# RWKV-7 and attention trunk: tiles for the first half's r mixes, the place of two loads, and the order inside a head norm

## The chip, the cores and the metric

One core of a Trainium2 chip runs the whole program. The metric is the device time of one execution in microseconds. The engines have their own instruction queues: PE (TensorE) multiplies matrices, DVE (VectorE), ACT (ScalarE) and POOL (GpSimd) work elementwise, SP (SyncE) issues most of the loads and stores. An engine works through its queue in order, so an instruction that waits holds up all that stand behind it.

## The reference, cut to what matters

Two layers over a sequence of S = 512 rows with D = 1024 features. Layer 0 is an RWKV-7 layer, and it is there that the change lies:

```
h = rms_norm(x)                       # h_prev is h shifted by one row
xr, xw, xk, xv, xa, xg = h + (h_prev - h) * mu[0..5]
r = xr @ w_r;  k = xk @ w_k;  v = xv @ w_v
w = -softplus(-(w0 + tanh(xw @ w1) @ w2)) - 0.5     # w1: 1024 x 64, w2: 64 x 1024
a = sigmoid(a0 + (xa @ a1) @ a2)                     # a1, a2 likewise
g = sigmoid(xg @ g1) @ g2
y = scan over the rows, 16 heads of 64, state 64 x 64 per head
y = head_norm(y) * lnx_w + lnx_b + bonus             # per head of 64: the "head norm"
x = x + (y * g) @ w_o
```

After it come a SwiGLU FFN, one shared K/V projection, a layer of differential attention and a second FFN. The change touches none of these.

## The kernel before, in words

Activations lie feature by feature on the partitions, as 8 tiles (kt = 0 to 7) of 128 features by 512 rows. The 16 heads are 8 pairs, and the layer works in two halves of four pairs: the first half's projections take columns 0 to 511 of a weight, the second half's the rest. A product in full precision is split in three: weight and activation are each cast to a high part (ACT) and a remainder (DVE), and TensorE adds high x high, low x high and high x low (L156 to L158).

The start: four loads of x (two on SP's queue, two on ACT's), squares (L265, L267) and a chain of additions on DVE (L272), a product with ones (L281), an inverse square root, the row factors (L254), and the normed h (L452). Also loaded there are `cst`, `lw` (lnx_w, broadcast over 128 partitions, 0.5 MB; on SP, L461, ahead of the first w_r load; it is read in the head norm, L904) and `sel` (on POOL's queue, L465).

The first stage merges four generators in turn (L480): the norming of h, the w product (into bank `ca`), the a product (into bank `cb`) and the first half of r (`r_half(0)`, which runs proj_p). Each of the last three needs its own mix of each feature tile: ACT scales h (L372), DVE adds the shifted h (L373). For w and a one fp32 product follows (L392, two instructions). For r, ACT casts the mix (L199), DVE makes the remainder (L200) and twelve products follow (L156 to L158, four banks). The weights of r come in four loads through one rotating `wr` buffer (the other two of three hold w1 and a1), with a cast L195 and a remainder L196 each. All mixes of this stage take the tag `xm`, which has two buffers: a mix waits until the mix two before it has been used. Mixes for k take the tag `xk`, which has nine.

The joint: when both products are done, ACT takes tanh of `ca` (L477) and copies both results (L399), DVE makes the remainders (L400), and TensorE multiplies by w2 and a2 (L414, L415), which ACT evicts (L538). Then the first half of k runs as proj_p again, with its own L195, L196, L199, L200.

After that a plan by numbers interleaves pairs, solve and the recurrence with the second halves of r, k and v. The recurrence hands over its output in tiles of 128 rows, four for each half; each of these eight gets a head norm (head_out, L879): mean and variance per head (L884 to L891, with the square on ACT, L888), inverse square root, weight and bonus (L904, L906), and then four turns of 128x128 (L911), each followed by its ACT copy with bias (L912), all in one PSUM bank `cb`. Behind the last of them the tail of the layer begins: DVE multiplies by g (L642), ACT casts (L646), DVE makes a remainder (L648), the weight w_o is cast (L662), and the last projection runs (L156).

A scheduler of the framework places instructions within each engine's queue; buffers and banks decide what waits.

Of the kernel before, what the change touches and what calls it, by code (L numbers as in the profile page):

```python
# [18 lines left out]
P = 128  # L19
D = 1024  # L20
# [22 lines left out]
class Trunk:  # L43
# [394 lines left out]
    def rwkv(self, turn):  # L438
        nc, A = self.nc, self.A
        xT = self.h  # L440
        rstd = self.norm_cols(xT, "pr", True)
        bc = self.rows_bc(rstd, "pr")
        cp = self.cp
        self.omu = cp.tile([P, 6 * KT], F32, name="omu")
        i0 = VI["mu0"] * KT
        nc.vector.tensor_scalar(self.omu, self.par[:, i0:i0 + 6 * KT], -1.0, 1.0, op0=ALU.mult, op1=ALU.add)
        h = xT

        def normed():
            for j in range(KT):  # L450
                v = h[j // 2][:, j % 2, :]
                nc.vector.scalar_tensor_tensor(out=v, in0=v, scalar=self.vec("g_mix0", j), in1=bc, op0=ALU.mult, op1=ALU.mult)  # L452
                yield
        self.h = h
        self.Dc = cp.tile([P, NP, NCH], F32, name="Dc")
        self.bon = cp.tile([P, NT, NP, 2], F32, name="bon")
        self.rkc = cp.tile([P, NP, 2], F32, name="rkc")
        for p in range(NP):
            nc.vector.tensor_scalar(self.rkc[:, p, :], self.cst[:, C_BO:C_BO + 2], self.vec("r_k", p), None, op0=ALU.mult)
        self.lw = cp.tile([P, D], F32, name="lw")  # L460
        nc.sync.dma_start(self.lw, A["lnx_w"].broadcast_to([P, D]))  # L461
        self.v_d = self.dr.tile([2, 2, S, 4, C], F32, name="v_d")
        self.st_d = self.dr.tile([2, NCH, P, 4, 8 * C], F32, name="st_d")
        self.sel = cp.tile([P, NT, P], F32, name="sel")
        nc.gpsimd.dma_start(self.sel, A["sel"])  # L465
        self.R, self.Pt, self.kept = {}, {}, {}
        self.oT = {}

        pwa = []

        def low(i):
            def out(ps):
                pwa or pwa.append(self.T("s", [P, 2, S], F32R))
                if i:
                    return self.halves(pwa[0][:, 1, :], ps)
                t = self.T("pr", [P, S])
                nc.scalar.activation(t, ps, AF.Tanh)  # L477
                self.halves(pwa[0][:, 0, :], t)
            return out
        self.merge(*zip((normed(), self.lora(h, 1, [(A["w1"], 2)], low(0), "ca"), self.lora(h, 4, [(A["a1"], 2)], low(1), "cb"), self.r_half(0)),  # L480
                        self.START))
        sg, aa = self.rates(pwa[0], 0)
        kr, ld, pg, sa, x1 = ([], []), ([], []), [], [(sg, aa)], []
        self.drain(self.k_half(0, kr[0]))

        def rates():
            sa.append(self.rates(pwa[0], 1))
            yield

        def out(w):  # L490
            if w == 0:
                x1.extend(self.load_x())
            yield from self.out_half(w, pg, x1)
        t = self.TIMES
        self.plan(
            [(lambda: self.pairs(0, kr[0], *sa[0], ld[0]), 20, *t["pairs0"]), (lambda: self.solve(0, *ld[0]), 36, *t["solve0"]),
             (lambda: self.rec(0), 24, *t["rec0"])],
            [(lambda: self.r_half(1), 8, *t["r1"]), (lambda: self.k_half(1, kr[1]), 8, *t["k1"]), (rates, 1, t["k1"][1], t["k1"][1]),
             (lambda: self.v_half(0), 8, *t["v0"]), (lambda: self.v_half(1), 8, *t["v1"]), (lambda: self.gate(pg), 8, *t["gate"]),
             (lambda: out(0), 9, *t["out0"])],  # L500
            [(lambda: self.pairs(1, kr[1], *sa[1], ld[1]), 20, *t["pairs1"]), (lambda: self.solve(1, *ld[1]), 36, *t["solve1"]),
             (lambda: self.rec(1), 24, *t["rec1"])])
        turn()
        self.drain(out(1))
        return x1

    def mixes(self, key, m, w):

        kept = self.kept.setdefault(key, {})

        def mix(kt):
            if key == "r":
                return self.mix_tile(self.h, m, kt)
            if w:
                return kept.pop(kt)
            x = kept[kt] = self.mix_tile(self.h, m, kt, "xk")
            return x
        return mix
# [360 lines left out]
    def head_out(self, w, tt, y):  # L879
        nc = self.nc  # L880
        w4 = w * 4
        yf = y.rearrange("p a b c -> p (a b) c")
        mean = self.tiny([P, 8])
        nc.vector.tensor_reduce(out=mean, in_=yf, axis=AX.X, op=ALU.add)  # L884
        nc.vector.tensor_scalar(mean, mean, 1.0 / C, None, op0=ALU.mult)
        self.lo("yf").tensor_tensor(out=yf, in0=yf, in1=mean.unsqueeze(2).to_broadcast([P, 8, C]), op=ALU.subtract)
        sq = self.T("ho", [P, 8, C])
        nc.scalar.activation(sq, yf, AF.Square)  # L888
        var = self.tiny([P, 8])
        nc.vector.tensor_reduce(out=var, in_=sq, axis=AX.X, op=ALU.add)  # L890
        nc.vector.tensor_scalar(var, var, 1.0 / C, 64e-5, op0=ALU.mult, op1=ALU.add)  # L891
        yield
        vt = self.T("ho", [P, 2, 4, C])
        for par in range(2):
            nc.sync.dma_start(vt[:, par], self.v_d[w, par, tt * P:(tt + 1) * P])
        for par in range(2):
            self.lo("vt").tensor_tensor(out=vt[:, par], in0=vt[:, par], in1=self.bon[:, tt, w4:w4 + 4, par:par + 1].to_broadcast([P, 4, C]), op=ALU.mult)
        rs = self.tiny([P, 8])
        self.rsqrt_v(rs, var, "ty")
        nc.vector.tensor_tensor(out=yf, in0=yf, in1=rs.unsqueeze(2).to_broadcast([P, 8, C]), op=ALU.mult)  # L900
        lv = self.lw[:, w * 512:w * 512 + 512].rearrange("p (a b c) -> p b a c", b=2, c=C)
        yo = sq.rearrange("p (a b) c -> p a b c", b=2)
        for par in range(2):
            nc.vector.tensor_tensor(out=y[:, par], in0=y[:, par], in1=lv[:, par], op=ALU.mult)  # L904

            nc.vector.tensor_tensor(out=yo[:, :, par, :], in0=y[:, par], in1=vt[:, par], op=ALU.add)  # L906
        yield
        ps = self.bank("cb")
        for i in range(4):
            p = w4 + i  # L910
            nc.tensor.transpose(ps[:, i * P:(i + 1) * P], yo[:, i].rearrange("p a b -> p (a b)"), self.ident)  # L911
            nc.scalar.activation(self.oT[p // 2][:, p % 2, tt * P:(tt + 1) * P], ps[:, i * P:(i + 1) * P], AF.Identity, bias=self.vec("lnx_b", p))  # L912

    def ffn(self, xT, l, tag, out=None):
# [367 lines left out]
```

## Time and profile before

| what | value |
|---|---|
| runs of the kernel, us | 1516.05, 1524.76, 1524.42 (median 1524.42) |
| profiled execution, us | 1518.63 |
| its span, us | 1516.8 |
| mean granted clock of TensorE | 0.984 |
| PE busy | 1447.9 us, 95% |
| DVE busy | 787.3 us, 52% |
| ACT busy | 529.1 us, 35% |
| POOL busy | 187.3 us, 12% |

The span runs from the first to the last record of the profiled execution. "Idle before" is the time in which the engine stood still ahead of an instruction, and the arrow names what ended it. The granted clock is 1.00 at 2.4 GHz and 0.50 at 1.2 GHz.

### The profile page before, as it was taken

How to read it: one execution, taken by the hardware profiler on the slowest of the kernel's cores; microseconds unless marked ns; L12 is line 12 of the kernel's file. 1: busy time of each engine (PE TensorE's matmuls, PEld its weight loads, DVE VectorE, ACT ScalarE, POOL GpSimd, SP SyncE). 2: the span in 40 equal slices, each digit the busy share in tenths (PEclk: the TensorE clock that was granted, in tenths of full speed). 3: DMA queues.
4: the chain of work that ended last, by engine and by line, in shares of the span. 5: the costliest groups of instructions: out<-in, count | busy, mean ns of one | idle time of the engine just before them, and what ended most of it. 6: DMA issues, size and time to landing. Idle time of an engine off the chain costs nothing.

```text
span 1516.8 us, 23107 instructions
## 1 busy us (share of the span) xinstructions
PE 1447.9 (95%) x9576; PEld 1140.0 (75%) x9576; DVE 787.3 (52%) x1511; ACT 529.1 (35%) x926; POOL 187.3 (12%) x156
## 2 busy tenths in 40 slices
PE   3899999999997999999999989999999999999998
PEld 2465555767685788888888879988778888888887
DVE  6735549677666644433323276666665444443222
ACT  4652341213423433222222153556654323232111
POOL 0002313100000111111100023111001111111000
PEclk9989999999998999999999999999999999999999
DMA  5112423776321322222222222111112232322231
GB/s 159 57 69 93 165 105 107 281 241 207 133 89 42 116 96 85 98 97 97 96 93 96 95 92 84 59 68 43 42 43 97 96 99 92 102 91 100 98 122 64
DMA packets 59162, 155.82 MB, mean 103 GB/s; under 512 B 12848, under 2 KB 19248, under 8 KB 57008
## 3 DMA queue, kind: packets, MB, share of 16 engines
q1 hardware_dynamic: 57856, 152.76, 29.3%
q8 instruction: 75, 1.23, 0.3%
q10 hardware_dynamic: 1120, 1.32, 0.3%
q14 instruction: 31, 0.25, 0.1%
q0 software_dynamic: 80, 0.26, 0.0%
HBM read 133.34 MB, written 20.97 MB: 102 GB/s over the span
## 4 chain that ended last, share of the span: by engine, by line
PE 83%; DVE 9%; ACT 3%; POOL 2%; issue 1%; DMA 1%; ACTq 0%; POOLq 0%
PE pj L156 15%; PE pj L157 15%; PE pj L158 15%; PE pj L182 3%; PE pj L216 3%; PE d L1058 2%; PE cb L875 2%; PE d L1060 2%; PE d L1059 2%; PE ca L833 2%; PE cb L743 1%; PE a L1156 1%; PE ca L157 1%; PE cb L157 1%; PE ca L158 1%
## 5 line engine op out<-in xcount | busy, mean ns | idle before, releaser
L150 ACT CAST wh<-wr 128x1024 fp32r<-128x1024 f32 x153 | 160.8, 1051 | 498.4 <-PE pj L157 224.2
L151 DVE TENSOR_TENSOR wl<-wr,wh 128x1024 fp32r<-128x1024 f32 x153 | 187.0, 1223 | 183.7 <-ACT wh L150 182.0
L156 PE MATMUL pj<-xa,wh 128*128 128x512 f32 x352 | 139.2, 395 | 1.3 <-ACT wh L150 1.3
L157 PE MATMUL pj<-xa,wh 128*128 128x512 f32 x352 | 138.9, 395 | 0.0
L158 PE MATMUL pj<-xa,wl 128*128 128x512 f32 x352 | 138.8, 395 | 0.0
L156 PE MATMUL pj<-xb,wh 128*128 128x512 f32 x352 | 137.1, 389 | 0.0
L158 PE MATMUL pj<-xb,wl 128*128 128x512 f32 x352 | 137.0, 389 | 0.0
L157 PE MATMUL pj<-xb,wh 128*128 128x512 f32 x352 | 137.0, 389 | 0.0
L945 POOL TENSOR_TENSOR hid<-ev,hid 128x512 fp32r<-128x512 f32 x44 | 68.2, 1551 | 403.6 <-ACT hid L944 403.6
L941 DVE TENSOR_TENSOR ev<-pj,bc 128x512 f32<-128x512 f32 x44 | 30.4, 691 | 144.5 <-PE pj L158 144.5
L938 DVE TENSOR_TENSOR ev<-pj,bc 128x512 f32<-128x512 f32 x44 | 30.4, 692 | 117.0 <-PE pj L158 114.7
L156 PEld LDWEIGHTS pj<-xa,wh 128*128 128x128 f32 x352 | 66.3, 188 | 17.4 <-ACT wh L150 2.2
L158 PEld LDWEIGHTS pj<-xa,wl 128*128 128x128 f32 x352 | 66.3, 188 | 15.7
L157 PEld LDWEIGHTS pj<-xa,wh 128*128 128x128 f32 x352 | 66.3, 188 | 15.3
L157 PEld LDWEIGHTS pj<-xb,wh 128*128 128x128 f32 x352 | 66.1, 188 | 13.8
L156 PEld LDWEIGHTS pj<-xb,wh 128*128 128x128 f32 x352 | 66.1, 188 | 13.7
L158 PEld LDWEIGHTS pj<-xb,wl 128*128 128x128 f32 x352 | 66.1, 188 | 13.6
L158 PE MATMUL pj<-hid,wl 128*128 128x512 f32 x176 | 68.5, 389 | 0.0
L156 PE MATMUL pj<-hid,wh 128*128 128x512 f32 x176 | 68.5, 389 | 0.0
L157 PE MATMUL pj<-hid,wh 128*128 128x512 f32 x176 | 68.5, 389 | 0.0
L216 PE MATMUL pj<-wr,xk 128*128 128x512 f32 x128 | 63.5, 635 | 0.0
L227 POOL TENSOR_TENSOR ty<-ty,mhalf 128x8 f32<-128x8 f32 (+1 forms) x20 | 35.4, 1770 | 157.6 <-DVE ty L1094 125.7
(337 smaller groups left out, 3124.7 us busy)
## 6 DMA issues: line engine op xcount, KB each, us to landing
wr<-in_wgu SPq DMA_DIRECT2D x88, 512.0 KB, 3.5
wr<-in_wdn SPq DMA_DIRECT2D x44, 512.0 KB, 3.5
st_d<-z SPq DMA_DIRECT2D x16, 1024.0 KB, 4.7
z<-st_d SPq DMA_DIRECT2D x16, 1024.0 KB, 6.3
wr<-in_w_kv SPq DMA_DIRECT2D x16, 512.0 KB, 3.6
wr<-in_w_r SPq DMA_DIRECT2D x8, 512.0 KB, 3.5
wr<-in_w_k SPq DMA_DIRECT2D x8, 512.0 KB, 3.5
wr<-in_w_v SPq DMA_DIRECT2D x8, 512.0 KB, 3.8
```

Of the source, the lines that this page charges most:

```text
L150: nc.scalar.copy(hi, raw)
L151: nc.vector.tensor_tensor(out=lo, in0=raw, in1=hi.bitcast(F32), op=ALU.subtract)
L156: mm(out, wh, xh, start=start, stop=False)
L157: mm(out, wh, xl, start=False, stop=False)
L158: mm(out, wl, xh, start=False, stop=stop)
L182: self.nc.tensor.matmul(pss[i], w[:, kt % 2, i * P:i * P + P], x, start=kt == kts[0], stop=kt == kts[-1])
L216: self.nc.tensor.matmul(pss[tt], x[:, tt * P:(tt + 1) * P], w[:, kt % 2, :], start=kt == 0, stop=kt == KT - 1)
L227: nc.gpsimd.tensor_tensor(out=y, in0=m, in1=half.to_broadcast(shp), op=ALU.pow)
L833: nc.tensor.matmul(ps[f, i * C:(i + 1) * C], L(f, i), R[f, i, :], start=False, stop=n == len(parts) - 1 and i == 3)
L938: nc.vector.tensor_tensor(out=a, in0=pss[0], in1=bc, op=ALU.mult)
L941: nc.vector.tensor_tensor(out=b, in0=pss[1], in1=bc, op=ALU.mult)
L945: nc.gpsimd.tensor_tensor(out=t[:, 1, :], in0=b, in1=t[:, 0, :].bitcast(F32), op=ALU.subtract)
```

## The change

Three edits. The r mixes of the first half take tiles of the tag `pr` (seven buffers, shared with the norm's temporaries) in place of `xm`; the w and a mixes keep `xm`, and so do the second half's r mixes. The `sel` load is written behind the first stage, and the `lw` load behind the first half of k. In the head norm, the four turns are written first and the four copies after them.

```diff
         self.lw = cp.tile([P, D], F32, name="lw")
-        nc.sync.dma_start(self.lw, A["lnx_w"].broadcast_to([P, D]))
...
         self.sel = cp.tile([P, NT, P], F32, name="sel")
-        nc.gpsimd.dma_start(self.sel, A["sel"])
...
         sg, aa = self.rates(pwa[0], 0)
...
+        nc.gpsimd.dma_start(self.sel, A["sel"])
         self.drain(self.k_half(0, kr[0]))
+        nc.sync.dma_start(self.lw, A["lnx_w"].broadcast_to([P, D]))
...
             if key == "r":
-                return self.mix_tile(self.h, m, kt)
+                return self.mix_tile(self.h, m, kt, "xm" if w else "pr")
...
         for i in range(4):
+            nc.tensor.transpose(ps[:, i * P:(i + 1) * P], yo[:, i].rearrange("p a b -> p (a b)"), self.ident)
+        for i in range(4):
             p = w4 + i
-            nc.tensor.transpose(ps[:, i * P:(i + 1) * P], yo[:, i].rearrange("p a b -> p (a b)"), self.ident)
             nc.scalar.activation(self.oT[p // 2][:, p % 2, tt * P:(tt + 1) * P], ps[:, i * P:(i + 1) * P], AF.Identity, bias=self.vec("lnx_b", p))
```

What the scheduler makes of it on the queues: the `sel` load stays the first load of POOL's queue. On SP's queue `lw` moves from ahead of the first w_r load to behind the two loads each of w1 and a1, and stays ahead of the second w_r load.

On PE's queue, in the first stage, one round of r stood as follows before (from the w and a products of one tile, `ca` and `cb`, to the first remainders; pj are r's four banks):

```order
L392 MATMUL ca_196<-xm_285,wr_193 128x512
L392 MATMUL cb_204<-xm_289,wr_201 128x512
L156 MATMUL pj_166<-z_297,z_296 128x512
L156 MATMUL pj_167<-z_297,z_296 128x512
L156 MATMUL pj_168<-z_297,z_296 128x512
L156 MATMUL pj_169<-z_297,z_296 128x512
L157 MATMUL pj_166<-z_297,z_296 128x512
L158 MATMUL pj_166<-z_297,z_296 128x512
```

and the same place of the changed kernel:

```order
L392 MATMUL ca_194<-xm_257,wr_191 128x512
L392 MATMUL cb_202<-xm_261,wr_199 128x512
L156 MATMUL pj_164<-z_237,z_236 128x512
L157 MATMUL pj_164<-z_237,z_236 128x512
L158 MATMUL pj_164<-z_237,z_236 128x512
L156 MATMUL pj_165<-z_237,z_236 128x512
L157 MATMUL pj_165<-z_237,z_236 128x512
L158 MATMUL pj_165<-z_237,z_236 128x512
```

The four products that need only the cast stood ahead of the eight others, and now each bank gets its three in a row, in every round.

On ACT's queue, at the joint (tanh, the two copies L399, the casts L199 of k's mixes and L195 of w_k's tiles), before:

```order
L199 CAST z_479<-xk_482 128x512
L477 ACTIVATE pr_414<-ca_196 128x512
L199 CAST z_479<-xk_499 128x512
L399 CAST s_413<-pr_414 128x512
L399 CAST s_413<-cb_204 128x512
L195 CAST z_518<-wr_516 128x1024
L538 ACT_TABLE_LOAD
```

and changed (where the tanh is at L475):

```order
L475 ACTIVATE pr_412<-ca_194 128x512
L195 CAST z_517<-wr_515 128x1024
L399 CAST s_411<-pr_412 128x512
L399 CAST s_411<-cb_202 128x512
L199 CAST z_518<-xk_521 128x512
L199 CAST z_518<-xk_538 128x512
L195 CAST z_557<-wr_555 128x1024
L538 ACT_TABLE_LOAD
```

The cast of w_k's second tile moved from behind the two copies to ahead of them, and two L199 and the cast of its third tile now stand ahead of the table load. On DVE's queue the second tile's remainder (L196) moved likewise from behind the two L400 to ahead of them.

On ACT's queue, in the tail of the second half (the copies of the last two head norms, `cb_4346` and `cb_4388`, the last norm's square L888, and the first casts behind the gate), before:

```order
L912 ACTIVATE s_3439<-cb_4346,par 128x128 x2
L888 ACTIVATE ho_4359<-ho_4101 128x512
L912 ACTIVATE s_3440<-cb_4346,par 128x128 x2
L912 ACTIVATE s_3439<-cb_4388,par 128x128 x2
L646 CAST s_4421<-xk_4419 128x512
L912 ACTIVATE s_3440<-cb_4388,par 128x128 x2
L646 CAST s_4421<-xk_4430 128x512
```

and changed (where the copy is at L913):

```order
L913 ACTIVATE s_3439<-cb_4346,par 128x128 x2
L913 ACTIVATE s_3440<-cb_4346,par 128x128 x2
L888 ACTIVATE ho_4359<-ho_4101 128x512
L913 ACTIVATE s_3439<-cb_4388,par 128x128 x2
L913 ACTIVATE s_3440<-cb_4388,par 128x128 x2
L646 CAST s_4421<-xk_4419 128x512
L646 CAST s_4421<-xk_4430 128x512
```

All four copies of a norm now stand together, the last norm's square behind all four of the norm before it, and the first cast behind all four of the last. On PE's queue the four turns of a norm likewise stand in a row, each time; of the four copies only the first waits for PE.

## Rows read from the trace of the kernel before

**Rows 1.** The page: the shares, by engine, of the chain of work that ended last.

```profile
PE 83%; DVE 9%; ACT 3%; POOL 2%; issue 1%; DMA 1%; ACTq 0%; POOLq 0%
```

**Rows 2.** The waits of PE over the whole span: what PE waited to run, the instruction that released it, us in total, times, longest.

```profile
PE cb L281 <- DVE pr L272: 17.8, 1, 17.8
PE pj L156 <- ACT z L199: 6.9, 5, 1.4
PE cb L911 <- DVE ho L906: 6.4, 2, 4.6
PE pj L156 <- ACT s L662: 4.0, 1, 4.0
...
PE pj L414 <- DVE s L400: 2.0, 1, 2.0
```

**Rows 3.** The timeline of PE, first stage: start and duration in us, engine, line, tiles, count, and in brackets the idle time before it.

```profile
52.23 1.19 PE L156 MATMUL pj<-z,z 128*128 128x512 f32 x4 [1.39 <-ACT z L199]
53.26 0.39 PE L157 MATMUL pj<-z,z 128*128 128x512 f32 x1
...
55.11 1.02 PE L392 MATMUL ca<-xm,wr 128*128 128x512 f32 x2
55.97 1.02 PE L392 MATMUL cb<-xm,wr 128*128 128x512 f32 x2
58.38 1.19 PE L156 MATMUL pj<-z,z 128*128 128x512 f32 x4 [1.39 <-ACT z L199]
```

**Rows 4.** The timeline of ACT, one round of the first stage.

```profile
56.17 1.58 ACT L372 ACTIVATE xm<-x,omu 128x512 f32<-128x512 f32 x2 [2.42 <-PE ca L392]
57.71 0.62 ACT L199 CAST z<-xm 128x512 fp32r<-128x512 f32 x1
```

**Rows 5.** Instructions of DVE by line between 25 and 75.3 us: count, busy us, mean ns, and idle time before them.

```profile
L373 DVE SCALAR_TENSOR_TENSOR xm<-x,par,xm 128x511 f32<-128x511 f32 x24 | 17.8, 749 | 9.0 <-ACT xm L372 8.5
L373 DVE SCALAR_TENSOR_TENSOR xk<-x,par,xk 128x511 f32<-128x511 f32 x9 | 6.5, 746 | 0.0
```

**Rows 6.** The timeline of DVE: the first normed tiles, and the last of the w and a mixes.

```profile
25.07 2.06 DVE L452 SCALAR_TENSOR_TENSOR x<-x,par,cb 128x512 f32<-128x512 f32 x3 [1.58 <-PE cb L254]
...
72.75 0.75 DVE L373 SCALAR_TENSOR_TENSOR xm<-x,par,xm 128x511 f32<-128x511 f32 x1
```

**Rows 7.** The DMA view of the first 20 us: the total, then issues by line, queue, count, KB each and median us from issue to landing.

```profile
DMA packets 6192, 4.96 MB, mean 248 GB/s; under 512 B 4592, under 2 KB 4720, under 8 KB 6192
...
lw<-in_lnx_w SPq DMA_DIRECT2D x1, 512.0 KB, 9.8
...
wr<-in_a SPq DMA_DIRECT2D x2, 256.0 KB, 4.4
```

**Rows 8.** The timeline of ACT at the start: the last of ACT's squares, released by the last load of x.

```profile
13.35 0.63 ACT L267 ACTIVATE pr<-x 128x512 f32<-128x512 f32 x1 [2.95 <-DMA x<-in_xT]
```

**Rows 9.** The timeline of PE from the end of the first stage into the first half of k.

```profile
74.42 1.02 PE L392 MATMUL cb<-xm,wr 128*128 128x512 f32 x2
77.45 0.51 PE L414 MATMUL pj<-s,ho 128*128 128x512 f32 x1 [2.01 <-DVE s L400]
...
80.46 0.74 PE L415 MATMUL pj<-s,ho 64*128 64x512 f32 x1
...
86.91 0.79 PE L156 MATMUL pj<-z,z 128*128 128x512 f32 x1
...
90.49 0.53 PE L158 MATMUL pj<-z,z 128*128 128x512 f32 x1
```

**Rows 10.** The timeline of ACT at the joint.

```profile
75.81 0.66 ACT L399 CAST s<-pr 128x512 fp32r<-128x512 f32 x1
76.33 0.63 ACT L399 CAST s<-cb 128x512 fp32r<-128x512 f32 x1
76.81 1.10 ACT L195 CAST z<-wr 128x1024 fp32r<-128x1024 f32 x1
```

**Rows 11.** The timeline of DVE at the joint.

```profile
76.71 0.69 DVE L400 TENSOR_TENSOR s<-pr,s 64x512 fp32r<-64x512 f32 x1
77.43 0.69 DVE L400 TENSOR_TENSOR s<-cb,s 64x512 fp32r<-64x512 f32 x1
78.15 1.23 DVE L196 TENSOR_TENSOR z<-wr,z 128x1024 fp32r<-128x1024 f32 x1
```

**Rows 12.** The timeline of SP's queue: the load of w_k's second tile.

```profile
72.87 0.33 SPq L142 DMA_DIRECT2D wr<-in_w_k  x1
```

**Rows 13.** The page, DMA issues: loads of w_k by count, KB each and median us from issue to landing.

```profile
wr<-in_w_k SPq DMA_DIRECT2D x8, 512.0 KB, 3.5
```

**Rows 14.** Windows, with TensorE's granted clock as the third number from the end: the end of the first stage, and the run behind it.

```profile
75.30:80.40 5.10, 3.09 (x8) 1.29 (x7) 3.67 (x5) 5.07 (x9) 0.00 (x0) 1.00 0.69 231
...
81.00:90.40 9.40, 9.40 (x17) 5.10 (x17) 1.99 (x3) 6.19 (x11) 0.00 (x0) 0.50 0.10 38
```

**Rows 15.** The timeline of ACT in the tail of the second half.

```profile
471.03 0.63 ACT L888 ACTIVATE ho<-ho 128x512 f32<-128x512 f32 x1
...
472.34 0.37 ACT L912 ACTIVATE s<-cb,par 128x128 f32<-128x128 f32 x1 [0.42 <-PE cb L911]
477.62 0.37 ACT L912 ACTIVATE s<-cb,par 128x128 f32<-128x128 f32 x1 [4.92 <-PE cb L911]
```

**Rows 16.** The timeline of DVE in the same tail.

```profile
478.02 0.69 DVE L642 TENSOR_TENSOR xk<-pj,s 128x512 f32<-128x512 f32 x1 [1.03 <-ACT s L912]
```

## The prediction

> **What bounds the kernel now.** The chain that ended last comes first: 83% of it is PE [rows 1], so time is won only where PE stands still. The waits of PE over the whole span list those places; the ones this change can reach [rows 2] are the head start (17.8 us behind the chain of additions), five waits of 1.4 us of r's first product for ACT's cast L199 (6.9 us), two waits of the head norm's turns (6.4 us), one behind the tail (4.0 us) and one at the joint (2.0 us). The timeline of PE then shows a round of the first stage [rows 3]: the first products of r start 1.39 us late at 52.23 and again at 58.38, 6.15 us apart. From 53.26 to 55.11 run the eight other products, 0.231 us each, then two pairs L392 of 0.86 us. Without the wait a round needs 12 x 0.231 + 2 x 0.86 = 4.49 us. ACT's timeline shows what is late [rows 4]: the mixes L372 start only when PE has finished the product on the older mix (2.42 us idle), because w, a and r share two buffers, and the cast L199 follows at 57.71, long after PE could have used it.
>
> **The change part by part.** *r's mixes in seven tiles.* They no longer wait for the w and a products, so ACT can cast them early and the five waits of 1.39 us go: **-6.9 us**. Two bounds. If PE then never pauses, five rounds shrink from 6.15 to 4.49 us, and the stage ends 8.3 earlier than 74.42 + 0.86 = 75.28 [rows 9]. Against that stands DVE. From its first normed tile at 25.07 to the end of its last w or a mix at 73.50 lie 48.4 us [rows 6], of which it stood idle 9.0 us ahead of mixes, nearly all for ACT's L372 [rows 5]. So it has 39.4 us of work, and one L200 more that the new order puts ahead of the last mix (0.6 us): never idle, it would end at 65.1 and PE one us later. PE and DVE would be almost equally full, which leaves little slack: DVE can spare 9.0 us of idle time, and if half of it stays, the gain is 4.5 us or less. I take the sum of the waits, which leaves DVE 2.3 us of idle time; the range of this term is -8.3 to -3.
>
> *The joint.* The stage would end at 68.4, the w product 0.86 earlier. The order at the joint is longer: tanh is now followed on ACT by the cast of w_k's second tile, which takes 1.04 us of its queue, then the two copies 0.52 us apart [rows 10]; on DVE that tile's remainder (1.2 us) stands ahead of the two L400, which are 0.72 us apart [rows 11]. Tanh from 67.6, cast from 68.1, copies from 69.1 and 69.6, remainder from 69.2 to 70.35, L400 to 71.8, and L414 there. Before, L414 stood at 77.45, 2.2 us behind the stage's end [rows 9]; now it is 3.4 behind: **+1.3 us**. Behind the waiting L414 the whole of the first half's k is queued on PE. The cast needs its weight: the load was issued at 72.87, when the first tile's remainder was done [rows 12], and lands 3.5 us later [rows 13]. In the new order that remainder stands three instructions (2.1 us) ahead of the end of the last mix, so at about 65, and the weight lands at 68.5 to 69: up to 0.9 us late, more if the mixes run late. It was behind the copies before and cost nothing. The range of this term is 0 to +3.5.
>
> *The clock behind the joint.* L414 and L415 ran 0.43 us apart until 80.46 and then 0.72 us, which is (86.91 - 80.46) / 9, at a granted clock of 0.50, which is 1.2 GHz; k's first nine products ran 0.43 us apart instead of 0.23, until 90.49 [rows 9, 14]. PE had just stood still 2.0 us. That cost 9 x 0.29 + 9 x 0.20 = 4.4 us. Here the pause is longer and the work ahead of it denser, so I let the clock fall again, a little earlier: **+0.5 us**, with -4.4 if it stays at 2.4 GHz, and +2.0 if all seven further products run at half.
>
> The Trainium skill bears on this: "TensorE: Matmul & The Clock Gate", Part 1, ties the granted rate to TensorE's recent activity. A denser first stage could by that rule keep the clock up; the rows here show that it fell after a pause of 2.0 us, and the fall is a case of its own below.
>
> *The late loads.* `sel` stays first on POOL's queue: nothing. `lw` moves on SP's queue behind w1 and a1. It is read in the head norms, hundreds of us later. What it can do is free the DMA engines for the last load of x, which lands at 13.35 and releases the chain of additions [rows 8, 2]. lw is 0.52 MB in pieces of 4 KB, 2.1 us at the mean of 248 GB/s; a1's two loads, now nearer, bring 0.52 MB in 4.4 us to landing [rows 7]. If a1's and w1's loads take the place of lw at their pace, the last x is 2.3 us later; if lw's bytes just leave the stretch, up to 1.4 us earlier. I take **-0.7**, since x comes over ACT's queue and only shares the engines.
>
> The Trainium skill speaks against it: "DMA: Bandwidth & Descriptors", section "Specifications", wants 512 bytes or more for the full rate, and w1 and a1 come in rows of 64 floats, 256 bytes. The trace agrees that most of the packets here are small, 4592 of 6192 under 512 bytes [rows 7]; by the rule the sum would be up to 3.0 us higher.
>
> *Four turns together.* At the tail of the second half this costs. The square L888 of the last norm ran at 471.03, between two pairs of copies; now it stands behind all four, the last of which ran at 472.34 [rows 15]: +1.3, and DVE's chain up to the last turns follows it. Then the first copy, at 477.62, waits for four turns instead of one: at 1.2 GHz three more of 0.2 us, +0.6, and the first product with the gate L642 at 478.02 [rows 16] waits for it. The end of the tail moves by **+1.9 us**; the copies that come sooner after one another (the last three waits of 0.5 us) help nothing, since the later L642 wait for the casts and remainders. At the other seven norms PE has products of its own beside them and waits only once more for the norm (6.4 - 4.6 = 1.8 us [rows 2]): zero, with -1.8 if that wait goes, and +2 if four turns in a row make other work wait.
>
> **The sum** is -0.7 - 6.9 + 1.3 + 0.5 + 1.9 = -3.9 us. The k stage behind the joint and the halves after it ran without a wait on these mixes, so they shift with it. The profiled execution took 1518.63 us, so 1514.7; the three runs lie around it (1516.05, 1524.76, 1524.42), the mean of the four is 1521.0, and I give **1517** by that.
>
> **The rivals.**
> *The clock stays up.* The stage keeps PE denser, and the fall behind the joint does not come: 4.4 won instead of 0.5 lost, -8.8, 1512. For it: the granted clock was 1.00 up to 80.40 in spite of the five waits. Against it: the pause at the joint gets longer.
> *Half the gain.* DVE, almost full, leaves PE waiting for mixes or remainders, or w_k's second tile lands late at the joint: 3 us kept instead of 6.9, or 3.5 paid instead of 1.3, sum about 0, 1521. For it: 40.0 us of DVE work in 42.
> *Slower.* The grouped turns hold up all eight head norms like the tail's square, 1.3 us each, 10.4 in all, against 5.8 us won before the tail (0.7 + 6.9 - 1.3 - 0.5): +4.6, 1526. It decides from five places on. Against it: PE waited for a norm at two places of eight [rows 2].
> *It does nothing.* r's cast is late for another reason than the two buffers: the rounds stay 6.15 us apart, and only joint and tail change, +2, 1523. Against it: the order has freed r's products of every wait inside a round, and ACT's idle time ends with PE's product.
>
> **How the numbers follow.** Forecast 0.55, clock up 0.13, half the gain 0.20, slower 0.07, nothing 0.05. The range from 1509 to 1523 takes in the first three and the spread of the runs; it leaves the slower case and the ends of the bounds out. For this kernel a change of about 1% (15 us) is what a measurement can tell from none. No case gains that much: faster 0.06 for several good bounds at once, slower 0.04, same 0.90.
>
> **What would show it.** In the changed profile: no wait of L156 for L199 in the first stage, its last L392 at about 68, a wait of about 3.4 us at L414 for L400, the granted clock at 0.50 behind it, L888 of the last norm about 1.3 us later against the turns before it, the first L642 about 0.6 us later after the last L906. The prediction is wrong if PE's waits in the first stage turn into waits for mixes (L392 for L373) of more than 3 us, if the last x lands later than 14, or if PE waits for turns or their copies at more than two of the norms.

## The result, and the profile after

The changed kernel took 1509.8 us (median of six runs, 1508.41 to 1513.69) against 1522.73 of the kernel before (six runs): a ratio of 0.9925, with a 95% interval of 0.99 to 0.9949. The two profiled executions took 1518.63 and 1508.41 us, 10.2 us apart, where the prediction had 3.9.

The waits of PE over the whole span of the changed kernel (what waited, what released it, us in total, times, longest) answer to [rows 2]:

```profile
PE cb L281 <- DVE pr L272: 16.7, 1, 16.7
PE pj L156 <- ACT s L662: 6.7, 1, 6.7
PE cb L910 <- DVE ho L906: 6.3, 2, 5.5
...
PE pj L414 <- DVE s L400: 2.7, 1, 2.7
...
PE ca L833 <- DVE rs L852: 1.7, 3, 0.8
...
PE ca L847 <- DVE rs L842: 1.3, 2, 0.9
```

The five waits of r's first product for L199 are gone. The head start is 1.1 us shorter. The joint and the tail wait longer, and the recurrence waits more for its small products (L833, which waited 0.4 us before, and L847, which did not wait). Waits alone don't tell where 10 us came from: PE's busy time fell from 1447.9 us to 1441.2 (on the pages of the two profiles), so of the 10.2 us by which the span is shorter only 3.5 were idle time of PE, and 6.7 were busy time, which no view of waits shows.

The timeline of PE in the first stage of the changed kernel answers to [rows 3], its last rows to [rows 9]:

```profile
50.59 1.02 PE L392 MATMUL ca<-xm,wr 128*128 128x512 f32 x2
51.45 1.02 PE L392 MATMUL cb<-xm,wr 128*128 128x512 f32 x2
...
55.07 1.02 PE L392 MATMUL ca<-xm,wr 128*128 128x512 f32 x2
...
64.91 1.02 PE L392 MATMUL cb<-xm,wr 128*128 128x512 f32 x2
68.67 0.50 PE L414 MATMUL pj<-s,ho 128*128 128x512 f32 x1 [2.74 <-DVE s L400]
...
69.97 0.79 PE L415 MATMUL pj<-s,ho 64*128 64x512 f32 x1
...
79.37 0.79 PE L156 MATMUL pj<-z,z 128*128 128x512 f32 x1
...
83.38 0.48 PE L156 MATMUL pj<-z,z 128*128 128x512 f32 x1
```

A round takes 55.07 - 50.59 = 4.48 us and has no idle time in it. The stage ends 9.5 us earlier than before (64.91 against 74.42), L414 8.8, k's first product 7.5: part of it is given back at the joint and behind it. The L414 run slows at 69.97, its fourth product, where it slowed at 80.46, its eighth, before.

DVE's waits between 24 and 64 us of the changed kernel, in the same columns, answer to [rows 5]:

```profile
...
DVE xm L373 <- ACT xm L372: 0.3, 1, 0.3
```

DVE's 9.0 us of idle time ahead of mixes have shrunk to 0.3, and it held up PE no more than before (one wait of 3.5 us of L392 for L373, at the start of the stage, in both kernels).

In the tail, ACT's timeline of the changed kernel answers to [rows 15]:

```profile
459.69 1.15 ACT L913 ACTIVATE s<-cb,par 128x128 f32<-128x128 f32 x4 [2.12 <-PE cb L910]
460.71 0.65 ACT L888 ACTIVATE ho<-ho 128x512 f32<-128x512 f32 x1
467.95 1.14 ACT L913 ACTIVATE s<-cb,par 128x128 f32<-128x128 f32 x4 [6.60 <-PE cb L910]
```

L888 waits behind the four copies, as foretold, but stands 10.3 us earlier than before (460.71 against 471.03). So more had been won by then than the 7.4 us that PE was ahead behind the joint.

Setting each product's start in the timeline of PE against its start in the kernel before gives the ledger. Each column is one execution's start less that of before, in us:

| product of PE (its start before) | changed | mixes only | loads only | turns only | mixes and loads |
|---|---|---|---|---|---|
| L281, head start (17.75) | -1.07 | 0.00 | -0.82 | +0.08 | -0.70 |
| L414, joint (77.45) | -8.78 | -7.31 | -0.75 | -0.38 | -8.36 |
| k's first L156 (86.91) | -7.54 | -6.38 | -0.91 | +0.11 | -7.15 |
| a product at 123 | -7.40 | -5.84 | -0.78 | -0.49 | -6.98 |
| a product at 312, ahead of the head norms | -7.22 | -4.02 | -1.12 | +3.45 | -6.77 |
| L156 behind the sixth norm (460.34) | -11.21 | -4.65 | -1.02 | -1.31 | -7.09 |
| first L156 of the tail (484.38) | -9.73 | -4.51 | -1.08 | +0.18 | -7.10 |
| a product at 1500 | -10.21 | -4.88 | -0.16 | -0.42 | -6.27 |

In the first column 4.0 us come between 312 and 460, where the prediction had put nothing. The other columns are the first four experiments.

### The profile page after: what moved, and what is told of

The parts are those of the page before. It is cut to its first block, busy times and chain, and to the rows that moved or that the text cites. A ratio compares the mean times of both kernels' runs of the same rounds, so it can differ in the third digit from the quotient of the medians.

```text
span 1506.6 us, 23120 instructions
## 1 busy us (share of the span) xinstructions
PE 1441.2 (96%) x9576; PEld 1138.9 (76%) x9576; DVE 785.1 (52%) x1511; ACT 525.9 (35%) x926; POOL 187.6 (12%) x156
## 4 chain that ended last, share of the span: by engine, by line
PE 83%; DVE 9%; ACT 3%; POOL 2%; issue 1%; DMA 1%; SPq 0%; ACTq 0%; POOLq 0%
PE pj L156 15%; PE pj L158 15%; PE pj L157 15%; PE pj L182 3%; PE pj L216 3%; PE d L1059 2%; PE d L1061 2%; PE d L1060 2%; PE cb L875 2%; PE ca L833 2%; PE cb L743 1%; PE a L1157 1%; PE ca L156 1%; PE cb L156 1%; PE ca L158 1%
## 5 line engine op out<-in xcount | busy, mean ns | idle before, releaser
L156 PE MATMUL pj<-xa,wh 128*128 128x512 f32 x352 | 139.2, 395 | 1.3 <-ACT wh L150 1.3
L156 PE MATMUL pj<-xb,wh 128*128 128x512 f32 x352 | 137.1, 389 | 0.0
L156 PEld LDWEIGHTS pj<-xa,wh 128*128 128x128 f32 x352 | 66.3, 188 | 17.4 <-ACT wh L150 2.2
L156 PEld LDWEIGHTS pj<-xb,wh 128*128 128x128 f32 x352 | 66.1, 188 | 13.8
L156 PE MATMUL pj<-hid,wh 128*128 128x512 f32 x176 | 68.5, 389 | 0.0
```

Source lines behind the costliest of these rows:

```text
L156: mm(out, wh, xh, start=start, stop=False)
```

## The experiments

### The three edits apart

Mixes only, in the kernel before:

```diff
-                return self.mix_tile(self.h, m, kt)
+                return self.mix_tile(self.h, m, kt, "xm" if w else "pr")
```

> Only the r mixes of the first half move to the seven tiles; both loads and the head norm stay as before. Theory A (the gain of the first stage is PE's alone, and the gain in the recurrence belongs to the grouped turns): the stage's last L392 starts about 8.3 us earlier than before (66.1 instead of 74.42), L414 about 7.7 earlier, k's first L156 about 6.4 earlier, and that shift of 6.4 us holds through the head norms to the end: time about 6.4 us below before. Rival B (the 4 us that the changed kernel wins between 320 and 460 us come from the earlier stage itself, by other phases of clock and loads): the shift grows to 9 to 11 us by 460 us. Start of the chain (L281) unchanged in both.

Loads only: the two `dma_start` of `lw` and `sel` moved as in the change, nothing else.

> Only the two loads are written later. Theory A: the last load of x lands about 1.1 us earlier (12.3 instead of 13.35), L281 follows at 16.7, and the whole rest shifts by 1.0 to 1.1 us and no more, since the rounds of the first stage stay 6.15 us apart. Rival B (small pieces of w1 and a1 alone speed or slow the start, the change in the changed kernel was chance of that execution): L281 within 0.3 us of 17.75, time as before.

Turns only: the four turns written ahead of the four copies, nothing else.

> Only the four turns are written ahead of their four copies. Theory A (each turn that stands apart among the small products of the recurrence costs PE about 0.2 us of pipeline at the change, so that four in a row save 0.6 to 0.9 us a norm): nothing moves before 320 us; behind it the shift grows in steps of 0.5 to 1 us at the norms to about -4 by 460, the tail gives 1.5 back, and the time ends 2 to 3 us below before. Rival B (grouping only costs, the square and the first copy come later): shift 0 up to the tail, then +1.5 to +2. Rival C (the gain was a clock fall avoided by chance at 391 us): a single step of about 1.3 us there.

Mixes and loads, turns and copies alternating as before:

> The changed kernel with turns and copies alternating as before: mixes and loads only. Theory A: shift 7.4 us behind the joint, the same 7.4 to the end, so 2.8 us slower than the changed kernel. Rival B (the gain in the recurrence belongs to the earlier stage): shift 10 us at the end, as in the changed kernel, or 11.5 without the tail's loss.

| kernel | median us | ratio to before | 95% interval |
|---|---|---|---|
| mixes only | 1514.84 | 0.9951 | 0.9934 to 0.9969 |
| loads only | 1518.64 | 0.9985 | 0.9971 to 0.9999 |
| turns only | 1515.72 | 0.9964 | 0.9944 to 0.9983 |
| mixes and loads | 1513.38 | 0.9945 | 0.9927 to 0.9964 |

All three edits win: 0.49%, 0.15% and 0.36%, together 1.0%, of which the changed kernel has 0.75%, with intervals that overlap. The ledger puts each gain where theory A said, though not each lasts: by 1500 us the mixes alone keep 4.9 of the 6.4 us that they had won at k's start, and the loads alone 0.2 of 0.9. The head start moves only with the loads (-0.82, -0.70). The recurrence moves only with the turns: between 312 and 460 the turns alone win 4.8 us, the changed kernel 4.0, mixes and loads 0.3, the mixes alone 0.6. The gain there is not one of the earlier stage (rival B), and not a single step (rival C), although one step is over half of it: at the fourth norm, from 388 to 400 us, the two kernels with grouped turns win 2.2 us. There PE's wait for L906 shrinks from 1.8 to 0.8 us, and the clock, which fell in the kernel before in that place (a mean granted clock of 0.66 from 390 to 395 us), stays at 1.00. The fifth and sixth norms win 0.6 and 0.8 us, and the first three, with the new waits, 0.3 together (all in the changed kernel).

What a group of turns saves is seen best where PE waits for nothing. The timeline of PE at the sixth norm, in the kernel with mixes and loads only (turns at L911):

```profile
447.91 0.28 PE L816 MATMUL ca<-zero,cst 128*128 128x256 bf16 x1
448.13 1.15 PE L833 MATMUL ca<-rs,z 64*64 64x64 f32 x32
449.21 0.33 PE L911 MATMUL cb<-cst,ho 128*128 128x128 f32 x1
449.37 0.27 PE L816 MATMUL ca<-zero,cst 128*128 128x256 bf16 x1
449.57 0.56 PE L833 MATMUL ca<-rs,z 64*64 64x64 f32 x10
450.06 0.33 PE L911 MATMUL cb<-cst,ho 128*128 128x128 f32 x1
450.32 0.38 PE L833 MATMUL ca<-rs,z 64*64 64x64 f32 x5
...
452.27 0.33 PE L911 MATMUL cb<-cst,ho 128*128 128x128 f32 x1
452.53 0.79 PE L875 MATMUL cb<-rs,z 64*64 64x64 f32 x10
453.25 0.50 PE L156 MATMUL pj<-s,s 128*128 128x512 f32 x1
```

and the same products in the changed kernel (turns at L910):

```profile
444.62 0.28 PE L816 MATMUL ca<-zero,cst 128*128 128x256 bf16 x1
...
445.92 0.66 PE L910 MATMUL cb<-cst,ho 128*128 128x128 f32 x4
446.41 0.27 PE L816 MATMUL ca<-zero,cst 128*128 128x256 bf16 x1
...
449.13 0.50 PE L156 MATMUL pj<-s,s 128*128 128x512 f32 x1
```

From L816 to L156 the same work takes 453.25 - 447.91 = 5.34 us with the turns apart and 4.51 in a group, 0.83 less, with no idle time shown in either. A lone turn holds the next small product back by 0.26 us (450.06 to 450.32; the four together 0.94), four in a row take 0.49 (445.92 to 446.41). That is 0.45 of the 0.83; for the rest the rows show that the small products, too, run in smaller groups between lone turns (L833 by 10 and 5, where the changed kernel has 16 at a time). What fits the whole is the number of changes between products of 128 rows (L816, the turns, L156) and of 64 rows (L833, L875): ten with the turns apart, four in a group, so 0.14 us for each of the six that are gone. The time sits inside "busy" PE, which is why no view of waits showed it; what a change costs the weight loads is shown below, with the full rows.

### Two turns at a time

```diff
-        for i in range(4):
-            nc.tensor.transpose(...)
-        for i in range(4):
-            p = w4 + i
-            nc.scalar.activation(...)
+        for j in (0, 2):
+            for i in (j, j + 1):
+                nc.tensor.transpose(...)
+            for i in (j, j + 1):
+                p = w4 + i
+                nc.scalar.activation(...)
```

> The changed kernel with the turns in two pairs: two turns, their two copies, two turns, two copies. Theory A (what counts is how often PE changes between turns and the small products, 0.35 us for a lone turn and 0.5 for four in a row): two changes a norm, about half of the 4 us of the recurrence are given back, 2 us slower than the changed kernel up to 460 us, the tail about 0.7 better. Rival B (the turns waited for the copies of their bank, and any grouping frees them): 4 us kept in the recurrence.

1512.46 us, a ratio of 0.994 (0.9922 to 0.9959) to before: a little slower than the changed kernel by its median, but the intervals overlap. Its profiled execution can't be compared as a whole, since between 123 and 312 us it lost 5.5 us, most of them to the clock (and 1.1 to longer waits for DVE at L757): in the windows view the granted clock (third number from the end) of its stretch from 200 to 225 us was

```profile
200.00:225.00 25.00, 25.00 (x69) 13.34 (x68) 9.36 (x34) 12.04 (x18) 4.86 (x4) 0.73 0.07 22
```

against 0.86 in the kernel before. From 312 to 460 us pairs win only 0.6 us where the changed kernel won 4.0, so rival B's whole gain did not come. Most of the difference is the fourth norm, where this execution also lost the clock (granted 0.50 from 390 to 395 us) that the changed kernel kept. At the fifth and sixth norms, where the changed kernel won 0.6 and 0.8 us, pairs gave back 0.3 and 0.2, a half and a quarter of it. At the sixth, pairs have six changes of row count where the changed kernel has four, 0.12 us for each of the two, which agrees with theory A's count of changes; whether pairs always lose the clock at the fourth norm, one execution does not show.

### The tail as before

The changed kernel, with `late = w == 1 and tt >= 2`, for which turns and copies alternate.

> The changed kernel, but in the last two head norms of the second half turns and copies alternate as before (the other six keep four in a row). Theory A (the grouped turns win in the recurrence and lose only in the tail, where the last norm's square L888 waits behind four copies and the first copy behind four turns): shift of about 11 us before the tail as in the changed kernel, L888 in its old place after L886, and 1.5 us more kept behind the tail: about 1.5 us faster than the changed kernel. Rival B (the grouping itself hurts nowhere; the tail's 1.5 us come from the clock): time as the changed kernel.

1508.47 us, a ratio of 0.9925 (0.9902 to 0.9949) to before: by measurement no better than the changed kernel. The trace shows the mechanism all the same. ACT's timeline of this kernel (copies at L914):

```profile
459.61 0.37 ACT L914 ACTIVATE s<-cb,par 128x128 f32<-128x128 f32 x1 [0.44 <-PE cb L910]
459.88 0.62 ACT L888 ACTIVATE ho<-ho 128x512 f32<-128x512 f32 x1
...
466.46 0.37 ACT L914 ACTIVATE s<-cb,par 128x128 f32<-128x128 f32 x1 [4.89 <-PE cb L910]
```

L888 and the first of the last copies are each earlier than in the changed kernel (460.71 and 467.95), and the tail's first L156 stands at 473.22 instead of 474.65. Of these 1.4 us, 0.6 were there already at 460; 0.9 are the tail's, not 1.5. The other 0.6 never reached the last norm's chain: L888 stands 11.15 us earlier than before (459.88 against 471.03) and the first L156 11.16, where PE at 460 was 11.77 ahead. PE waits 4.8 us for L906 there, so the norm's chain, and not PE, sets the time.

### What the clock behind the joint depends on

Three filler products of 0.86 us, in the changed kernel, between the first stage and the L414 run:

```diff
                         self.START))
+        fill = self.bank("ca")
+        for _ in range(3):
+            nc.tensor.matmul(fill, self.ident, h[0][:, 0, :], start=True, stop=True)
```

> The changed kernel with three more products of 128x512 fp32 (0.86 us each, into a bank that nothing reads) in the pause between the last product L392 and the first L414, so that PE stands still there about 0.2 us instead of 2.7. Theory C (the granted clock falls behind the joint because PE pauses there): L414 and L415 all 0.43 us apart, k's first products 0.23, k starts 2.9 us earlier, and the kernel gets about 4.5 us faster. Rival D (the clock falls because of the run of L414 and L415 itself, whose products stand 0.43 us apart at 2.4 GHz where r's stand 0.23): it falls to 0.50 all the same, later by no more than a few us; gain 0 to 2 us.

Full rows: the remainder's product over 128 rows, the upper 64 made zero.

```diff
+        nc.vector.tensor_scalar(lo[C:P], raw[C:P], 0.0, None, op0=ALU.mult)
...
-            nc.tensor.matmul(ps, lo[0:C, c], x[0:C], start=False, stop=True)
+            nc.tensor.matmul(ps, lo[:, c], x, start=False, stop=True)
```

> The changed kernel, with the remainder's product L415 taken over 128 rows instead of 64 (its upper 64 rows are zeros, made by one more DVE instruction per load), so that all products of that run have one shape. It computes the same. Rival D (the run of L414 and L415 is thin because the row count changes at every product and the weight load can't go beside the product before): the spacing becomes 0.23 us, as far as ACT's evictions of 0.62 us per two products let it, the clock does not fall or comes back sooner, k's first L156 starts 3 to 5 us earlier; a little at the second run near 200 us too. Theory C (the pause alone decides): spacing 0.43 and the fall stay, time as the changed kernel or 0.6 us more for DVE's extra work.

The filler kernel took 1507.51 us (0.9907 of before, 0.9886 to 0.9929), full rows 1499.7 (0.9861, 0.9843 to 0.988). PE's timeline with the filler:

```profile
65.03 2.74 PE L482 MATMUL ca<-x,cst 128*128 128x512 f32 x6
68.00 0.50 PE L414 MATMUL pj<-s,ho 128*128 128x512 f32 x1 [0.23 <-DVE s L400]
...
71.94 0.79 PE L415 MATMUL pj<-s,ho 64*128 64x512 f32 x1
...
77.00 0.79 PE L156 MATMUL pj<-z,z 128*128 128x512 f32 x1
```

PE now pauses 0.23 us instead of 2.74, and the clock falls all the same, at 71.94, the tenth product of the run instead of the fourth. The pause is not the only cause. With full rows (products at L415 and L416):

```profile
69.30 0.80 PE L415 MATMUL pj<-s,ho 128*128 128x512 f32 x1 [3.85 <-DVE s L400]
69.89 0.63 PE L416 MATMUL pj<-s,ho 128*128 128x512 f32 x1
...
75.42 0.40 PE L415 MATMUL pj<-s,ho 128*128 128x512 f32 x1
75.66 0.39 PE L416 MATMUL pj<-s,ho 128*128 128x512 f32 x1
75.89 0.39 PE L156 MATMUL pj<-z,z 128*128 128x512 f32 x1
```

After a pause of 3.85 us the run starts at half the clock, but 0.43 us apart where it was 0.72, and by 75.42 it has 0.23, which k keeps: k starts at 75.89 instead of 79.37. Row counts that alternate between 128 and 64, then, cost twice: 0.43 us a product where 0.23 would do, and a run that loses the clock. The second such run, near 200 us, shows it without any pause ahead (PE is busy for all of the 25 us from 200 to 225 in the kernel before, at a mean granted clock of 0.86): spaced 0.43 before, 0.23 with full rows (L415 at 194.47, L416 at 194.71), no fall of the clock (the 16 products of two columns between the run's halves are in both kernels), and 5.2 us more of shift behind it (-13.41 us at 200, -18.65 at 250).

Why the spacing doubles, the timeline of the weight loads shows (PEld, which loads the stationary operand of each product; "issue" stands where the profile shows nothing that was waited for). In the second run of the changed kernel, with one product between two loads:

```profile
201.20 0.18 PEld L415 LDWEIGHTS pj<-s,ho 64*128 64x128 f32 x1 [0.24 <-issue]
201.20 0.49 PE L415 MATMUL pj<-s,ho 64*128 64x512 f32 x1
201.62 0.19 PEld L414 LDWEIGHTS pj<-s,ho 128*128 128x128 f32 x1 [0.24 <-issue]
```

with full rows (L415 is here the product of the high part), and in the changed kernel's products of 96 rows, which stand between products of 128:

```profile
194.71 0.19 PEld L415 LDWEIGHTS pj<-s,ho 128*128 128x128 f32 x1
194.94 0.39 PE L415 MATMUL pj<-s,ho 128*128 128x512 f32 x1
...
457.44 0.19 PEld L435 LDWEIGHTS pj<-s,pr 96*128 96x128 f32 x1
457.67 0.39 PE L435 MATMUL pj<-s,pr 96*128 96x512 f32 x1
```

At a change between 128 and 64 rows the load starts only with its own product; otherwise it runs beside the product before, 0.23 us ahead. All 252 such changes in the kernel before, and all 229 in the changed one, have the load at most 5 ns ahead, those around the turns among the 64x64 products too. So both findings come down to the same change, and not every alternation has this price: 128 and 96 rows alternate at 0.23 us. Why the load waits at the one change and not at the other, no run here shows.

### All three together

The changed kernel with the tail as before, full rows and four fillers; and the same with the zeros made by POOL (`nc.gpsimd.tensor_scalar`).

> The changed kernel with the tail's two norms alternating as before, the remainder's product over 128 rows, and four filler products (3.4 us, into a bank that nothing reads) in the pause at the joint. If the clock behind the joint falls for two reasons, the pause and the thin run of L414 and L415, then with both gone it stays at 2.4 GHz: products of that run 0.23 us apart where ACT's evictions allow (0.62 us per two, behind a table load of 1.3), k's first L156 about 2 us earlier than with the full rows alone; with 1.0 us from the tail it is some 3 us faster than with the full rows alone, near 1497. If the filler only delays the run (its L400 come first or the evictions bound it), it equals the full rows alone, less the tail's 1 us.

> The same as the kernel with all three, except that the zeros of the upper rows are made by POOL instead of DVE. If DVE, nearly full in the first stage, sets the end of the stage, the two instructions taken from it (0.6 us each) bring the stage's last L392 about 1 us earlier; if PE sets it, the stage's end and L400 move by less than 0.3 us.

All three took 1498.05 us, a ratio of 0.9852 (0.9823 to 0.988): the fastest here by its median, 1.65 us below full rows alone and inside their intervals. PE's timeline:

```profile
65.39 3.60 PE L483 MATMUL ca<-x,cst 128*128 128x512 f32 x8
69.31 0.50 PE L415 MATMUL pj<-s,ho 128*128 128x512 f32 x1 [0.32 <-DVE s L400]
...
72.84 0.50 PE L415 MATMUL pj<-s,ho 128*128 128x512 f32 x1 [1.42 <-ACT s L542]
...
75.16 0.50 PE L156 MATMUL pj<-z,z 128*128 128x512 f32 x1
```

and its windows over the same stretch (the granted clock is the third number from the end):

```profile
70.00:75.00 5.00, 3.58 (x15) 2.02 (x13) 3.03 (x4) 4.97 (x9) 0.00 (x0) 1.00 0.52 179
75.00:80.00 5.00, 5.00 (x23) 4.01 (x22) 2.04 (x3) 3.57 (x7) 0.00 (x0) 1.00 0.04 16
```

Either cause alone made the clock fall (filler: the run; full rows: the pause); with both gone it stays at 1.00 through the joint, in this execution and in that of the next kernel. Only 0.7 us of it reach k's start (75.16 against 75.89), since the wait moves on: after four banks PE waits 1.42 us for ACT's first eviction. And they did not last: at 123 us the kernel stands 1.6 us behind full rows alone (-11.87 us to before, against -13.47), because its clock fell later (granted 0.50 from 104 to 108 us, where full rows alone had 1.00).

With the zeros on POOL it took 1499.29 us (0.9864, 0.9826 to 0.9902), and the stage ended later, not earlier. POOL's and ACT's timelines of that kernel:

```profile
54.35 3.93 POOL L411 TENSOR_SCALAR ho<-wr 64x512 fp32r<-64x512 f32 x1 [4.84 <-DMA wr<-in_a]
...
61.77 1.05 ACT L195 CAST z<-wr 128x1024 fp32r<-128x1024 f32 x1 [4.11 <-DMA wr<-in_w_k]
```

POOL takes 3.9 us here (1.5 to 1.9 the other three times) for what DVE did in 0.42 (median, full rows), and holds the `wr` buffer as long; the load of w_k that needs it goes out at 58.31 instead of 57.00, ACT waits for it at L195, and the last mix behind that cast reaches PE 1.25 us late. Neither of the two answers written ahead fits: what became critical is the buffer.

## Why the prediction came out as it did

The direction was right and the time, 1509.8, lies in the range, 0.8 us above its lower end; the gain was 2.6 times the forecast (10.2 us between the profiled executions, 12.9 between the medians, 3.9 foretold). That the range held is in part luck: it reached so low for the rival that the clock stays up (1512) and for the spread of the runs, and the clock fell. As foretold, the change stays under 1%. Term by term, in us, from the first column of the ledger:

| term | foretold | measured | from |
|---|---|---|---|
| start | -0.7 | -1.1 | L281 |
| first stage | -6.9 | -8.4 | last L392, -9.51, less the start |
| joint | +1.3 | +0.7 | L414, -8.78 |
| clock behind it | +0.5 | +1.4 | -7.40 at 123 |
| head norms but the tail's | 0 | -4.0 | -7.22 at 312, -11.21 at 460 |
| tail | +1.9 | +1.5 | -9.73 |
| the rest (123 to 312, behind the tail) | 0 | -0.3 | -7.22 and -10.21 |
| sum | -3.9 | -10.2 | |

**The step that failed** is "at the other seven norms PE has products of its own beside them and waits only once more for the norm: zero". It counted waits alone. PE pays for a turn among the 64x64 products also where it waits for nothing, 0.6 and 0.8 us at the fifth and sixth norms, and the turns alone win 4.8 us between 312 and 460 while mixes and loads win 0.3. The one wait that the prediction named there, 1.8 us at the fourth norm, shrank by 1.0 where the sum had it unchanged, and the clock that did not fall behind it brings that place to 2.2 us. New waits of the small products (L833 and L847, 3.0 us against 0.4) took part of it back.

**The first stage** was right in its mechanism and sized too small. I took the sum of the waits, 6.9, because DVE seemed too full for more, and gave half the gain a chance of 0.20. The bound by PE came true: five rounds of 6.15 us became rounds of 4.48, which is 8.35 of the 8.4. Of the 1.67 us that a round lost, the view of waits had shown 1.39; the rest was busy time here too. DVE's work was sized well: 24.01 to 63.81 is 39.8 us, where the prediction had 40.0. That it could run with almost no idle time (0.3 us before mixes) was the part not believed. The full-rows kernel puts two more instructions on DVE and starts its last L392 at 64.42, no later than the changed kernel.

**The joint** was foretold in its mechanism: tanh, L195, two L399, L196 and two L400 in that order, and a wait 0.7 longer instead of 1.3. The sum had L414 start behind both L400, but the rows before show it behind the first one ([rows 11]: 76.71 + 0.69 = 77.40, and L414 at 77.45 in [rows 9]); with that its own working puts L414 at 71.1, which is +0.5. w_k's second tile was in time for the joint; the first made ACT wait 1.9 us at L195 and DVE 0.65 at L196, which did not reach PE.

**The clock** fell as foretold, earlier than foretold (fourth product instead of eighth), and cost 0.9 more. The prediction gave the pause as its cause; the filler showed that the run itself does it too. The rival "the clock stays up" did not happen in the changed kernel. It did with filler and full rows, and there only 0.7 us of it reached k's start, since the joint's wait moved to ACT's evictions.

Of the Trainium skill's "TensorE: Matmul & The Clock Gate", Part 1, the runs agree that the granted rate follows recent activity: 1.00 through the joint with filler and full rows, 0.50 without. The Trainium skill's rule from "DMA: Bandwidth & Descriptors", section "Specifications", against small pieces did not decide the start: with w1 and a1 ahead of lw, x's last tile landed 1.1 us earlier, and the loads alone give 0.15%. (The upper bound of 1.4 us on this term has no working in the prediction.)

**The tail** was right: 1.5 instead of 1.9, with L888 behind four copies (0.9 us instead of 1.3: 10.3 us ahead of before where PE was 11.2) and the first copy behind four turns (0.65 instead of 0.6).

The slower rival had the grouped turns hold up all eight norms; they held up the tail's and helped at the fourth to sixth. The sums of two rivals were loose and decided nothing: the late w_k tile alone (3.5 instead of 1.3) gives -1.7 and not 0, and joint and tail alone (1.3 and 1.9) give +3.2 and not +2. The rival that nothing changes fell with the first round.

## What to carry to other kernels

A view of waits shows what an engine waits for, not what it pays when it changes between shapes: when a change puts like products side by side, time the same stretch of work from its first to its last product, before and after. Products whose row counts alternate between 128 and 64 cost twice here, in their spacing and in the clock, while 128 and 96 cost nothing; filling the smaller with zeros was worth 0.7% (1499.7 against 1509.8 by the medians), nearly as much as the whole change. And a buffer's last reader, not only its first, belongs into the price when work is moved to a slower engine.

## What was not expected of the hardware

One 128-row product among 64-row ones holds PE for about a quarter of a microsecond with no idle time shown; four of them apart cost 0.83 us more at one norm than in a row. At every change between 128 and 64 rows the weight load started with its own product and not beside the one before; at a change between 128 and 96 it ran beside it.

The granted clock fell with PE never idle (0.86 from 200 to 225 us of the kernel before), in a run whose products stood 0.43 us apart at 2.4 GHz. Behind a pause it came back within the same run of sixteen products when they had full rows (by 75.42, the run having begun at 69.30), and only in k's products (83.38, the run having begun at 68.67) when they had not.

Executions of nearly the same program differ by up to 5.5 us between 123 and 312 us, mostly by the granted clock (0.86, 0.80 and 0.73 from 200 to 225 us in the kernel before, turns only and turn pairs), which is more than the loads or the turns are worth by themselves; only the ledger by place, not the total of one execution, told them apart.
